# A two-layer hybrid attention stack: log gates by tokens, another order of heads and of competing PE lines

## Chip, cores, metric

One core of a Trainium2 chip. The metric is the device time of one execution in microseconds (us), median of the runs taken; the kernel before was run three times.

## The reference

Two layers over 1040 tokens (16 meta tokens and 1024 of `x`, width 1024, fp32). Each layer normalises the residual stream, projects it to 3588 columns and mixes three branches:

```python
log_f = log_sigmoid(fg + b_f[l])                    # forget gates, 4 heads
c = cumsum(log_f, axis=1)
a_out = forgetting_attention(fq, fk, fv, c) * silu(fz)      # scores + c[q] - c[k], causal
b_out = rmsnorm(differential_attention(dq, dk, dv, lam), subln_g[l]) * (1 - lambda_init) * silu(dz)
c_out = pooling_mixer(pu, w_pool[l], pool_scale[l]) * silu(pz)   # means of 2, 4, 8, 16 tokens
h = h + concat(a_out, b_out, c_out) @ w_out[l]
```

There are four forget heads of 64 columns and four difference heads (two score maps each, softmaxes subtracted with a factor `lam`). The output is `rmsnorm(h[16:], final_g)`.

## The kernel before

Every product is made of fp32r halves (a rounded part and the rest) in two or three matmuls, so PE does three passes for a projection. A layer runs as a stream of projections (`projections`, `proj_chunk`, three column chunks of about 346 tokens) in which the attention of six **units** is woven: two forget pairs (units 0 and 1, two heads each) and four difference heads (2 to 5). `UNITS` (L38) gives their order. While the attention of one unit runs, the V, Q and K projections of the next unit and the gate Z of this one are computed; in the last unit's time the two pooling items (`pool_item`, `pooling`) and their gates stand in the list `more` (L1525 to L1535).

The normalised tokens are transposed by PE (`to_hnT`, L584) into the tile `HT`. At the start `load_x` loads the token tiles (`x`), `load_g` the norm's factors (`g`), `rms` multiplies by both, and `forget_gates` (L722) computes the gates of layer 0 from `HT` with the split weights `wg`. For layer 1 the gates are made token by token in `next_gates` (L743): DVE multiplies each normalised row with the four gate columns `gw`, the sums land in `gt` (128 tokens x 9 x 4), nine PE transposes bring them into the row tile `gx` (4 partitions x 1040), and `gate_sums` (L773) takes the logarithm of the sigmoid and the running sum on those 4 partitions: minimum, a combination, Exp, Ln, a subtraction, a memset, a scan. The sums go to DRAM (`c_d`), and each forget pair reads its two rows back, broadcast to 128 partitions (`cb`).

What sets the order of the work: all operations but the PE's lines are recorded by `Timed` (so nearly all rows of ACT, DVE, POOL and SP bear L151), and `Order` lists them again. PE has up to six lines (`stream`: projections, scores, sums, transposes of V, start), each in fixed order; `Order.simulate` picks at every step, for every engine, the instruction that can start first by a table of costs (`Order.cost`), with the longest remaining way as a tie-break, and `Order.tell` writes that order into the program. On each engine instructions then run strictly in that order, and SP's queue (the DMA issues) too. PSUM has two banks `psP` for projections, three `psS` for scores, two `psT` for transposes, one `psO`. The SBUF ring `row` has eight buffers for `cb`, `sz`, `rq`, long softmax rows `p` and others.

`pooling` (L1189) makes window sums on DVE (`wa`, `wb`, `hd`), `pool_mix` (L1215) multiplies with `wps` on PE and evicts with the scale `sc`, a small DMA of its own. `meta_t` (L1002) copies the meta part of a weight block into `ptm`: ACT, DVE, ACT.

## Time and profile before

| | us |
|---|---|
| median of 3 runs (1224.27 to 1226.64) | 1224.74 |
| the profiled execution | 1224.48 |
| its span | 1222.7 |
| PE busy | 1188.7 (97%) |
| DVE, ACT, POOL busy | 814.0, 658.3, 493.5 |

The span is what the profiler shows from the first to the last instruction; the profiled execution is 1.8 us longer. PE's busy time counts a matmul from its start to a modelled end, so short delays between matmuls don't show as idle time, and idle time of other engines costs nothing by itself. The granted clock of PE was 0.998 of full speed over the span.

### The profile page before, as it was taken

What the parts mean: (1) busy time and instruction counts of PE and PEld (TensorE: products, weight loads), DVE (VectorE), ACT (ScalarE), POOL (GpSimd) and SP (SyncE); (2) the same over time, 40 slices, a digit from 0 to 9 for tenths busy, and PEclk for the clock granted to TensorE, in tenths of its full rate; (3) what the DMA queues carried; (4) which work ended last, traced back from release to release, by engine and by line L of the source; (5) the groups of instructions that cost most, each with busy time, mean ns of one, the idle gap of its engine ahead of it and who ended that gap; (6) DMA issues with size and microseconds to landing.
All of it is one profiled execution on the core that took longest, in us unless ns stands there. A gap on an engine that the chain in (4) does not pass through costs nothing.

```text
span 1222.7 us, 21035 instructions
## 1 busy us (share of the span) xinstructions
PE 1188.7 (97%) x7605; PEld 1120.7 (92%) x7605; DVE 814.0 (67%) x2137; ACT 658.3 (54%) x1536; POOL 493.5 (40%) x572
## 2 busy tenths in 40 slices
PE   5999999999999999899999999999999999999997
PEld 4999999999999999878889899999999999998886
DVE  6557567675766767667886675676768585777422
ACT  6556556565555654552235565665655555556322
POOL 4331623336162542465425234252443526235532
PEclk9999999999999999999999999999999999999999
DMA  7120211121222263472110212111223223325431
GB/s 244 27 71 18 59 47 27 45 44 32 53 40 61 35 126 78 136 237 80 67 53 18 71 36 69 27 27 53 30 42 61 40 50 65 78 50 158 140 108 52
DMA packets 101273, 84.21 MB, mean 69 GB/s; under 512 B 18296, under 2 KB 90232, under 8 KB 101168
## 3 DMA queue, kind: packets, MB, share of 16 engines
q1 hardware_dynamic: 101024, 82.60, 26.5%
q8 instruction: 60, 0.98, 0.3%
q14 instruction: 45, 0.37, 0.1%
q10 hardware_dynamic: 144, 0.26, 0.1%
HBM read 69.00 MB, written 13.80 MB: 68 GB/s over the span
## 4 chain that ended last, share of the span: by engine, by line
PE 86%; DVE 5%; ACT 3%; DMA 2%; issue 2%; SPq 1%; POOL 1%; POOLq 0%; ACTq 0%; DVEq 0%
PE psP L517 55%; PE psS L517 15%; PE psO L517 8%; PE psT L523 7%; DVE p L151 1%; SPq L151 1%; DMA r_d<-rs 1%; PE psS L523 1%; PE psT L517 1%; ACT K L151 1%; DVE K L151 1%; DMA sc<-in_pool_scale_dram 1%; ACT ptm L151 0%; DMA x<-in_x_dram 0%; DVE ptm L151 0%
## 5 line engine op out<-in xcount | busy, mean ns | idle before, releaser
L517 PE MATMUL psP<-HT,ws 128*128 128x346 f32 (+5 forms) x4032 | 730.3, 325 | 3.9 <-DVE K L151 2.0
L517 PEld LDWEIGHTS psP<-HT,ws 128*128 128x128 f32 x4032 | 636.5, 188 | 6.5 <-issue 2.3
L151 POOL TENSOR_TENSOR ws<-wr,ws 128x512 fp32r<-128x512 f32 x112 | 150.0, 1342 | 263.3 <-ACT ws L151 203.0
L151 POOL TENSOR_TENSOR q<-rq,q 64x256 fp32r<-64x256 f32 (+1 forms) x192 | 147.9, 770 | 124.7 <-DVE q L151 104.2
L151 ACT ACTIVATE p<-p,mx 128x144 f32<-128x144 f32 (+3 forms) x192 | 150.5, 784 | 49.3 <-DVE mx L151 48.3
L517 PE MATMUL psS<-K,q 128*128 128x392 f32 (+9 forms) x696 | 146.7, 324 | 1.0 <-DVE mx L151 0.8
L151 DVE TENSOR_TENSOR pp<-psT,pp 128x512 fp32r<-128x512 f32 (+1 forms) x160 | 99.2, 634 | 46.7 <-ACT pp L151 45.0
L517 PE MATMUL psO<-pp,VV 128*128 128x256 f32 (+1 forms) x800 | 129.2, 283 | 0.2
L523 PE MATMUL psT<-identf,p 128*128 128x128 f32 (+1 forms) x704 | 114.5, 273 | 3.3 <-DVE p L151 3.0
L151 ACT ACTIVATE pp<-psT 128x512 fp32r<-128x512 f32 (+1 forms) x160 | 85.4, 551 | 60.0 <-PE psT L523 55.9
L517 PE MATMUL psP<-HT,ms 128*128 128x512 f32 (+1 forms) x504 | 115.0, 385 | 0.5 <-POOL ms L151 0.3
L517 PEld LDWEIGHTS psO<-pp,VV 128*128 128x128 f32 x800 | 113.1, 189 | 2.0 <-DVE pp L151 0.9
L517 PEld LDWEIGHTS psS<-K,q 128*128 128x128 f32 (+1 forms) x696 | 108.4, 186 | 4.7 <-DVE mx L151 2.7
L517 PEld LDWEIGHTS psP<-HT,ms 128*128 128x128 f32 x504 | 90.7, 188 | 20.7 <-POOL ms L151 0.8
L523 PEld LDWEIGHTS psT<-identf,p 128*128 128x128 f32 (+1 forms) x704 | 81.3, 132 | 10.8 <-DVE p L151 4.7
L151 ACT ACTIVATE ws<-wr 128x512 fp32r<-128x512 f32 x112 | 70.0, 628 | 33.4 <-PE psP L517 18.4
L151 ACT ACTIVATE ptm<-psT 32x256 fp32r<-32x256 f32 (+1 forms) x128 | 47.5, 371 | 63.1 <-DVE ptm L151 45.0
L517 PE MATMUL psS<-HT,ms 128*128 128x512 f32 (+2 forms) x320 | 75.4, 394 | 0.0
L151 DVE TENSOR_SCALAR p<-p,rd 128x144 f32<-128x144 f32 (+7 forms) x128 | 72.3, 568 | 1.7
L517 PEld LDWEIGHTS psS<-HT,ms 128*128 128x128 f32 (+2 forms) x320 | 57.5, 180 | 16.7
L151 DVE TENSOR_TENSOR K<-psP,K 64x346 fp32r<-64x346 f32 (+1 forms) x72 | 37.2, 517 | 47.4 <-ACT K L151 46.8
L151 POOL TENSOR_TENSOR ms<-mr,ms 128x128 fp32r<-128x128 f32 (+2 forms) x39 | 39.1, 1010 | 68.7 <-ACT ms L151 68.6
(138 smaller groups left out, 1423.0 us busy)
## 6 DMA issues: line engine op xcount, KB each, us to landing
wr<-in_w_in_dram SPq DMA_DIRECT2D x112, 256.0 KB, 2.8
wo<-in_w_out_dram SPq DMA_DIRECT2D x14, 512.0 KB, 5.3
mr<-mix_d SPq DMA_DIRECT2D x14, 320.0 KB, 4.5
cb<-c_d SPq DMA_DIRECT2D x8, 520.0 KB
x<-in_x_dram SPq DMA_DIRECT2D x8, 512.0 KB, 6.5
res<-in_x_dram SPq DMA_DIRECT2D x8, 512.0 KB
h_d<-res SPq DMA_DIRECT2D x8, 512.0 KB, 2.6
res<-h_d SPq DMA_DIRECT2D x8, 512.0 KB, 4.6
```

Of the source, the lines that this page charges most:

```text
L151: r = f(*args, **kw)
L517: r = nc.tensor.matmul(o, w, m, start=start, stop=stop)
L523: r = nc.tensor.transpose(o, src, ident)
```

## The change

- In `next_gates` (layer 1) the logarithm is taken on the token-major tile `gt` (128 x 36) ahead of the transposes: bias, minimum, combination, Exp, Ln, subtraction. Only the scan stays on 4 x 1040, its ones are a constant, and the bias `bf` is loaded broadcast to 128 partitions. `gate_sums` still serves layer 0.
- The first `x` tile is asked for ahead of `g` (`load_x(2)` ahead of `load_g`).
- `UNITS` becomes (0, 2, 1, 3, 4, 5): a difference head between the two forget pairs, in both layers.
- In the last unit's list the first pooling item stands ahead of the unit's gate, the second behind it.
- `Order`: where PE's lines compete, the head that would be ready 400 ns (`SPARE`) later is compared, not the earliest; the scan's cost is 2.1 ns an element; writes to `ptm` count as writes to the whole tile, and in `meta_t` both ACT copies now stand ahead of the DVE subtraction; the list is made six times with new remaining ways, and the one that ends first by the table is kept (`choose`).

```diff
--- before.py
+++ after.py
@@ -35,7 +35,7 @@
 SLOPES = (2.0 ** -2, 2.0 ** -4, 2.0 ** -6, 2.0 ** -8)
 CHUNKS = ((0, 348), (348, 346), (694, 346))
 OWN_CHUNKS = (CHUNKS, ((META, 348 - META), *CHUNKS[1:]))
-UNITS = (0, 1, 2, 3, 4, 5)
+UNITS = (0, 2, 1, 3, 4, 5)
 V_CHUNKS = ((0, 400), (400, 384), (784, 256))
 FQ, FK, FV, FZ, FG = 0, 256, 512, 768, 1024
 DQ, DK, DV, DZ = 1028, 1540, 2052, 2564
@@ -166,6 +166,8 @@
 
     HOP = {"pe": 200, "act": 38, "dve": 38, "pool": 38, "dma": 0}
 
+    SPARE = 400
+
     def __init__(self):
         self.ops, self.writes, self.reads, self.rings, self.place = [], {}, {}, {}, {}
         self.stream = 0
@@ -208,7 +210,7 @@
                 name = ap.tensor.name
                 names.add(name)
                 p0, p1, at = self.parts(ap)
-                if self.place.get(name, ("",))[0] == "VM":
+                if self.place.get(name, ("",))[0] in ("VM", "ptm"):
                     p0, p1, at = 0, 128, [(0, 1 << 20)]
                 for lo, hi in at:
                     for other in others:
@@ -250,7 +252,9 @@
             return 158 + 1.05 * n + 63 * pointers, False
         if op == "reciprocal":
             return 157, False
-        if not sbuf or op == "tensor_tensor_scan":
+        if op == "tensor_tensor_scan":
+            return 150 + 2.1 * n, True
+        if not sbuf:
             return 150 + 1.05 * n, False
         if op == "tensor_copy" or op == "tensor_scalar":
             if len(ins[0].ap) > len(out.ap) or any(d[0] == 0 for d in ins[0].ap):
@@ -274,25 +278,36 @@
         for o in ops:
             for b in o["before"]:
                 ops[b]["after"].append(o["k"])
-
-        last = None
-        for o in reversed(ops):
-            way = max((ops[a]["way"] for a in o["after"]), default=0.0)
-            for n in o["tiles"]:
-                tag, i = self.place[n]
-                bufs, names = self.rings[tag]
-                if i + bufs < len(names) and self.first[names[i + bufs]] > o["k"]:
-                    way = max(way, ops[self.first[names[i + bufs]]]["way"])
-            way += o["end"]
+        self.start, self.heir = None, {}
+        for bufs, names in self.rings.values():
+            self.heir.update(zip(names, names[bufs:]))
+
+    def weigh(self):
+
+        ops, last = self.ops, None
+        for o in reversed(ops if self.start is None else sorted(ops, key=lambda o: (self.start[o["k"]], o["k"]))):
+            after = o["after"] + [self.first[self.heir[n]] for n in o["tiles"] if n in self.heir]
+            way = max((ops[a].get("way", 0.0) for a in after), default=0.0) + o["end"]
             if o["eng"] == "pe":
                 if last is not None:
                     way = max(way, last + o["dur"])
                 last = way
             o["way"] = way
 
+    def choose(self, rounds):
+
+        self.prepare()
+        best = None
+        for _ in range(rounds):
+            self.weigh()
+            end = self.simulate()
+            if best is None or end < best[0]:
+                best = end, self.start, self.done, self.taken, self.order
+            self.heir = {old: n for n, old in self.taken.items() if old}
+        _, self.start, self.done, self.taken, self.order = best
+
     def simulate(self):
         ops = self.ops
-        self.prepare()
         left = [len(o["before"]) for o in ops]
         ready = [0.0] * len(ops)
         start, done = [None] * len(ops), [None] * len(ops)
@@ -347,11 +362,13 @@
                         if not line or left[line[-1]] or (s := slots(line[-1])) is None:
                             continue
                         t = max(free["pe"], ready[line[-1]] + 20, s + 20)
-                        d = (t, 0.0, line[-1], t, e)
+                        sure = max(free["pe"], ready[line[-1]] + self.SPARE, s + self.SPARE)
+                        d = (sure, 0.0, line[-1], t, e)
                         if c is None or d < c:
                             c = d
                     if c is None:
                         continue
+                    c = (c[3], *c[1:])
                 else:
                     c = None
                     for k in waiting[e]:
@@ -742,14 +759,14 @@
 
     def next_gates(l):
 
-        bf = small.tile([4, 1], F32, tag="bf", name=nm("bf"), bufs=2)
-        sync.dma_start(bf, b_f[l].rearrange("(f o) -> f o", o=1))
-        gx = row("gx")[:4]
+        bf = small.tile([128, 4], F32, tag="bfr", name=nm("bf"), bufs=1)
+        sync.dma_start(bf, b_f[l].partition_broadcast(128))
         gw = [sb.tile([128, D], F32, tag="q", name=nm("gw"), bufs=4) for _ in range(4)]
         for f in range(4):
             sync.dma_start(gw[f], c_wg[l, f].partition_broadcast(128))
 
         gt = small.tile([128, 9, 4], F32, tag="gt", name=nm("gt"), bufs=1)
+        dve.memset(gt, 0.0)
         done = []
 
         def rows(hn, np_, col):
@@ -761,12 +778,24 @@
             done.append((g, np_, col))
 
         def end():
+            gx = row("gx")[:4]
+            flat = gt.rearrange("p n f -> p (n f)")
+            mn = sm("mn", 36)
+            dve.tensor_tensor(out=gt, in0=gt, in1=bf.unsqueeze(1).to_broadcast([128, 9, 4]), op=ALU.add)
+            dve.tensor_scalar(out=mn, in0=flat, scalar1=0.0, scalar2=None, op0=ALU.min)
+            dve.scalar_tensor_tensor(out=flat, in0=mn, scalar=2.0, in1=flat, op0=ALU.mult, op1=ALU.subtract)
+            act.activation(flat, flat, AF.Exp)
+            act.activation(flat, flat, AF.Ln, bias=1.0)
+            dve.tensor_tensor(out=flat, in0=flat, in1=mn, op=ALU.subtract)
             with ordr.line(4):
                 for g, np_, col in done:
                     pt = psT()[:4, :np_]
                     transpose(pt, g, identf[:np_, :np_])
-                    act.activation(gx[:, col : col + np_], pt, AF.Identity, bias=bf)
-            gate_sums(l, gx)
+                    act.activation(gx[:, col : col + np_], pt, AF.Copy)
+            mn = row("mn")[:4]
+            dve.tensor_tensor_scan(
+                out=mn, data0=one[:4].to_broadcast([4, T]), data1=gx, initial=0.0, op0=ALU.mult, op1=ALU.add)
+            sync.dma_start(c_d[l], mn)
 
         return rows, end
 
@@ -1007,8 +1036,8 @@
                 transpose(pt[:, b + 128 * i : b + 128 * i + 128], P[2 * jp + i][:, 0:32], identf)
             ptm = keep["m"] = small.tile([96, 272], F32R, tag="ptm", name=nm("ptm"), bufs=2)[:, :nq]
             act.activation(ptm[0:32], pt, AF.Copy)
+            act.activation(ptm[64:96], pt, AF.Copy)
             dve.tensor_tensor(out=ptm[32:64], in0=pt, in1=f32(ptm[0:32]), op=ALU.subtract)
-            act.activation(ptm[64:96], pt, AF.Copy)
 
         def out_tile():
             if "O" not in keep:
@@ -1464,6 +1493,7 @@
         act.dma_start(out[0, t0 : t0 + 128, 512:], res[:, 512:])
 
     HT = big.tile([128, 2, 8, T], F32R, name="HT")
+    load_x(2)
     g = load_g(norm_g[0])
     load_x(5)
     hns = []
@@ -1530,7 +1560,7 @@
                 more += nxt
             else:
                 Y = []
-                more += [pool_item(l, t, Y) for t in (1, 0)] + [pool_gate(l, t, Y) for t in (1, 0)]
+                more = [pool_item(l, 1, Y), *more, pool_item(l, 0, Y)] + [pool_gate(l, t, Y) for t in (1, 0)]
                 raw = []
                 more[-1] = (*more[-1][:4], lambda: (w_out_loads(l, raw, 4), raw.append(first_mix(l))))
             unit_steps(cur, end, len(more) * tile_ns + (LAG if u == 5 else 0))
@@ -1546,7 +1576,7 @@
         plan.run(op, 14 * 3 * 216)
         for _ in op:
             pass
-    ordr.simulate()
+    ordr.choose(6)
     ordr.tell(tc)
 
 _INS = ("x", "meta_tokens", "norm_g", "w_in", "b_f", "lam_q1", "lam_k1", "lam_q2", "lam_k2",
```

What this does to the order, at three places.

**The start, PE** (matmuls of the gate chunk of layer 0 write psP_296; `identf,x_104` and `identf,x_157` are transposes of the fourth and fifth token tile; `psP_330` is the first V chunk). Before:

```order
L523 MATMUL psS_282<-identf,x_104 128x128 x4
L523 MATMUL psS_289<-identf,x_104 128x128 x4
L523 MATMUL psS_316<-identf,x_157 128x128 x2
L517 MATMUL psP_296<-HT,wg_138 36x348 x16
L523 MATMUL psS_316<-identf,x_157 128x128 x2
L523 MATMUL psS_323<-identf,x_157 128x128 x4
```

Now:

```order
L540 MATMUL psS_282<-identf,x_104 128x128 x4
L540 MATMUL psS_289<-identf,x_104 128x128 x4
L534 MATMUL psP_296<-HT,wg_138 36x348 x16
L534 MATMUL psP_330<-HT,ws_149 128x400 x12
L534 MATMUL psP_330<-HT,ws_154 128x400
L540 MATMUL psS_316<-identf,x_157 128x128 x4
L540 MATMUL psS_323<-identf,x_157 128x128 x4
```

The gate chunk no longer stands behind two transposes of the fifth tile. On **DVE** at the same place, before:

```order
L151 TENSOR_TENSOR HT<-psS_275,HT 128x4x128
L151 CAST wg_138<-wrg_139 128x8x4
L151 SCALAR_TENSOR_TENSOR x_157<-x_157,rs_177,g_96 128x1024
L151 TENSOR_TENSOR wg_138<-wrg_139,wg_138 128x8x4
L151 TENSOR_TENSOR HT<-psS_282,HT 128x4x128
L151 TENSOR_TENSOR HT<-psS_289,HT 128x4x128
```

Now:

```order
L151 SCALAR_TENSOR_TENSOR x_104<-x_104,rs_166,g_98 128x1024
L151 CAST wg_138<-wrg_139 128x8x4
L151 TENSOR_TENSOR wg_138<-wrg_139,wg_138 128x8x4
L151 TENSOR_TENSOR HT<-psS_282,HT 128x4x128
L151 TENSOR_TENSOR HT<-psS_289,HT 128x4x128
L151 SCALAR_TENSOR_TENSOR x_157<-x_157,rs_177,g_98 128x1024
```

The split of `wg` moved ahead of the normalisation of the fifth tile `x_157`; that of the fourth, `x_104`, moved behind two more subtractions for `HT`.

**Layer 1's gates, DVE** (mn, na, gx: the row tiles of `gate_sums`; K0, K1: eviction of a K chunk from psP). Before:

```order
L151 TENSOR_SCALAR mn_7967<-gx_6828 4x1040
L151 SCALAR_TENSOR_TENSOR na_7969<-mn_7967,gx_6828 4x1040
L151 TENSOR_TENSOR K_1666_8034<-psP_8082,K_1666_8034 64x346
L151 MEMSET gx_6828 4x1040
L151 TENSOR_TENSOR K_1667_8035<-psP_8082,K_1667_8035 64x346
L151 TENSOR_TENSOR na_7969<-na_7969,mn_7967 4x1040
L151 TENSOR_TENSOR K_1666_8034<-psP_8111,K_1666_8034 64x346
L151 SCALAR_TENSOR_TENSOR mn_7967<-gx_6828,na_7969 4x1040
L151 TENSOR_TENSOR K_1667_8035<-psP_8111,K_1667_8035 64x346
```

Now (gt: the token-major tile; the row with `one` is the scan):

```order
L151 SCALAR_TENSOR_TENSOR gt_6836<-mn_7941,gt_6836 128x36
L151 TENSOR_TENSOR gt_6836<-gt_6836,mn_7941 128x36
L151 CAST q_7987<-rq_7685 64x256 x2
L151 CAST q_7996<-rq_7685 64x256 x2
L151 TENSOR_TENSOR K_1666_8035<-psP_8047,K_1666_8035 64x348
L151 TENSOR_TENSOR K_1667_8036<-psP_8047,K_1667_8036 64x348
L151 TENSOR_TENSOR VV_7683<-psT_8054,VV_7683 128x2x64 x2
L151 SCALAR_TENSOR_TENSOR mn_7975<-one,gx_7940 4x1040
L151 TENSOR_TENSOR K_1666_8035<-psP_8083,K_1666_8035 64x346
L151 TENSOR_TENSOR K_1667_8036<-psP_8083,K_1667_8036 64x346
L151 CAST q_8005<-rq_7685 64x256 x2
```

Of the 4 x 1040 operations the scan alone is left, and it stands ahead of the second K chunk instead of inside the third.

**The pooling of layer 0, SP** (sc: the scale of a pooling item; r_d and vr: a trip of norm factors through DRAM; wo: output weights). Before:

```order
L151 DMA wp_6486<-in_w_pool_dram 64x64 x2
L151 DMA r_d<-rs_1367_6270 128x2
L151 DMA wo_6767<-in_w_out_dram 128x512
L151 DMA vr_6346<-r_d 128x256
L151 DMA sc_6343<-in_pool_scale_dram 128x1
L151 DMA sc_6493<-in_pool_scale_dram 128x1
L151 DMA wo_6768<-in_w_out_dram 128x512
```

Now, the first scale:

```order
L151 DMA wr_6084<-in_w_in_dram 128x4x128
L151 DMA wr_6089<-in_w_in_dram 128x4x128
L151 DMA sc_6063<-in_pool_scale_dram 128x1
L151 DMA wr_6414<-in_w_in_dram 128x4x128
L151 DMA wr_6419<-in_w_in_dram 128x4x128
```

and the second:

```order
L151 DMA vr_6322<-r_d 128x272
L151 DMA r_d<-rs_1367_6268 128x2
L151 DMA wo_6767<-in_w_out_dram 128x512
L151 DMA vr_6356<-r_d 128x256
L151 DMA sc_6493<-in_pool_scale_dram 128x1
L151 DMA wo_6768<-in_w_out_dram 128x512
```

The first scale stands ahead of the weights of the pooling gates, far ahead of the trips through r_d; the second still stands behind one.

## Rows read from the trace of the kernel before

**Rows 1.** Page, first part: busy time of each engine, share of the span, instructions.

```profile
PE 1188.7 (97%) x7605; PEld 1120.7 (92%) x7605; DVE 814.0 (67%) x2137; ACT 658.3 (54%) x1536; POOL 493.5 (40%) x572
```

**Rows 2.** Busy time by stretch: length, busy PE, PEld, DVE, ACT, POOL (instructions), granted clock, DMA.

```profile
19.00:22.40 3.40, 0.57 (x5) 0.36 (x4) 3.40 (x4) 2.52 (x5) 3.24 (x4) 1.00 0.58 167
...
22.40:26.60 4.20, 4.20 (x18) 2.76 (x18) 1.03 (x2) 0.63 (x1) 2.60 (x3) 0.59 0.72 198
...
40.00:490.00 450.00, 447.69 (x3043) 435.66 (x3042) 308.28 (x940) 262.32 (x622) 176.22 (x186) 1.00 0.23 52
...
490.00:550.00 60.00, 56.44 (x329) 48.13 (x327) 36.98 (x73) 34.04 (x83) 33.52 (x40) 1.00 0.61 186
...
672.00:690.00 18.00, 15.72 (x105) 15.04 (x103) 8.83 (x23) 9.53 (x21) 5.60 (x4) 1.00 0.34 105
...
690.00:1085.00 395.00, 392.97 (x2682) 383.45 (x2681) 280.30 (x814) 233.18 (x544) 149.88 (x166) 1.00 0.22 47
...
1085.00:1120.00 35.00, 32.71 (x219) 31.82 (x218) 25.96 (x58) 20.34 (x41) 16.29 (x15) 1.00 0.38 106
...
1120.00:1222.70 102.70, 96.03 (x456) 79.27 (x454) 36.42 (x49) 31.06 (x82) 38.21 (x65) 0.99 0.35 109
```

**Rows 3.** Timeline of the first 40 us: start, length, engine, operation, count, idle before.

```profile
5.76 1.27 DVE L151 SCALAR_TENSOR_TENSOR x<-x,rs,g 16x1024 f32<-16x1024 f32 x1 [3.72 <-DMA g<-in_norm_g_dram]
...
7.09 1.06 ACT L151 ACTIVATE junk<-x 128x1024 bf16<-128x1024 f32 x1 [3.15 <-DMA x<-in_x_dram]
...
10.10 4.69 PE L523 MATMUL psS<-identf,x 16*128 16x16 f32 x24 [10.10 <-DMA identf<-in_ident_dram]
...
18.80 1.07 DVE L151 CAST wg<-wrg 128x32 fp32r<-128x32 f32 x1
...
19.78 2.35 DVE L151 SCALAR_TENSOR_TENSOR x<-x,rs,g 128x1024 f32<-128x1024 f32 x1
...
22.27 0.51 PE L523 MATMUL psS<-identf,x 128*128 128x128 f32 x2 [2.83 <-DVE wg L151]
...
22.44 4.33 PE L517 MATMUL psP<-HT,wg 128*36 128x348 f32 x16
...
37.13 2.74 PE L517 MATMUL psP<-HT,wg 128*36 128x346 f32 x16
```

**Rows 4.** Timeline around layer 1's gates: DVE, then PE.

```profile
673.84 1.23 DVE L151 TENSOR_TENSOR na<-na,mn 4x1040 f32<-4x1040 f32 x1 [2.78 <-ACT na L151]
...
675.64 2.31 DVE L151 TENSOR_TENSOR_SCAN mn<-gx,na 4x1040 f32<-4x1040 f32 x1
...
678.65 7.53 PE L517 MATMUL psP<-HT,ws 128*128 128x346 f32 x46 [2.03 <-DVE K L151]
```

**Rows 5.** Chain that ended last, 660 to 700 us: start, length, piece.

```profile
679.47 2.42 DMA c_d<-mn
...
681.91 4.02 DMA cb<-c_d
```

**Rows 6.** Chain that ended last, 490 to 530 us.

```profile
488.31 5.26 DMA r_d<-rs
...
494.00 2.91 DMA sc<-in_pool_scale_dram
```

**Rows 7.** Timeline at the two pooling stages: PE, then DVE and PE.

```profile
497.73 0.75 PE L517 MATMUL psP<-pu,wps 128*128 128x346 f32 x3 [1.21 <-ACT Y L151]
...
511.18 1.86 PE L517 MATMUL psP<-HT,ws 128*128 128x348 f32 x10 [1.53 <-DVE th L151]
...
1104.35 4.14 DVE L151 SCALAR_TENSOR_TENSOR p<-p,n,p 128x912 f32<-128x912 f32 x2
...
1108.55 0.55 PE L523 MATMUL psT<-identf,p 128*128 128x128 f32 x3 [1.83 <-DVE p L151]
```

**Rows 8.** Waits of the whole span: who for whom, us in total, times, longest.

```profile
ACT ptm L151 <- DVE ptm L151: 45.0, 63, 1.8
...
PEld psO L517 <- ACT ptm L151: 4.2, 13, 0.5
```

## The prediction

> **What bounds the kernel now.** I read the page's first part first: PE is busy for 1188.7 of 1222.7 us, the next engine (DVE) for 814.0 [rows 1]. Before and after the change PE has the same products and transposes to do, so the only time to be had is PE's idle time, 1222.7 − 1188.7 = 34.0 us, and what PE does at the lower clock. The second view is busy time by stretch, to see where those 34.0 us lie [rows 2]. 10.1 us come before the first transpose [rows 3]; the stretch 19.0 to 22.4 lacks 2.83; the two attention stretches 40 to 490 and 690 to 1085 lack only 2.31 and 2.03 in 845 us together; the end of layer 0 (490 to 550) lacks 3.56, layer 1's gates (672 to 690) 2.28, the end of layer 1 (1085 to 1120) 2.29, and the tail from 1120 lacks 6.67. The change touches the tail in nothing. So what it can reach is 2.83 + 3.56 + 2.28 + 2.29 = 10.96 us at the four seams, some 4.3 inside the attention, and the clock in the head. Third I read the timeline at the four seams [rows 3, 4, 7], for what each wait waits for; fourth the chain of waits, for the DMAs behind them [rows 5, 6]; last the waits of the whole span, for the work on `ptm` [rows 8].
>
> The sum is made against the profiled execution, 1224.48 us, 1.8 above its span and 0.3 below the median of the runs. A measurement of this kernel can tell about 0.2% (2.4 us) from no change.
>
> **Part by part.**
>
> *x ahead of g: 0.* The first rows are multiplied at 5.76, when `g` lands; the first full tile of `x` lands only for 7.09. Now the two change places, so `g` should come some 7.09 − 5.76 = 1.3 later and `x` earlier by as much. But PE's first transposes start at 10.10 because of `identf` [rows 3], which stands behind the same transfers in either order. The multiplication of 16 rows takes 1.27; begun at 7.1 it ends at 8.4, still 1.7 ahead of `identf`, which is the cover. If that were gone, it would cost the 1.3 at most.
>
> *The gate chunk of layer 0 comes earlier: −2.0 (bounds −2.8 and −0.7).* PE waits 2.83 us up to 22.27, by the profile for `wg` (the split by DVE); then it does two transposes of the fifth tile and the 16 gate matmuls [rows 3]. The cast of `wg` ends at 18.80 + 1.07 = 19.87, and only behind it stands the multiplication of `x_157`, 2.35 long, 19.78 to 22.13: the second half of `wg`, and `x_157` itself, wait for that. In the new order both operations on `wg` stand ahead of `x_157`, and PE's gate chunk ahead of its transposes. The second half of the split is 128 x 32; the nearest price is the cast of the same tile, 1.07; anything from near 0 to that. So the gate chunk could start between 19.9 and 21.0 in place of 22.44. The multiplication of the fourth tile, `x_104`, now stands closer ahead of the split (nearest row: 1.27), so it could be put off by 1.27 more. Lower bound 22.44 − 20.94 − 0.8 = 0.7, upper 2.8 (the whole wait); I take 2.0, nearest to a short second half. What is gained stays gained: from 22.4 to 26.6 PE is busy without a gap (4.20 of 4.20).
>
> *Layer 1's gates: −2.2 (bounds −2.5 and −1.0).* On DVE the 4 x 1040 subtraction (1.23, which first idled 2.78 for ACT's Ln) and the scan (2.31) stand among the evictions of K; PE waits 2.03 at 678.65 for the last of them [rows 4]. Now combination, Exp, Ln and subtraction are 36 wide, and the memset is gone; the scan is left, one chunk earlier and without a wait for ACT in front of it. New are a memset of `gt`, an addition with a stretched operand, and the bias loaded to 128 partitions, all well ahead and small: I set them at 0 under PE's products before 672 (PE is busy 15.72 of 18.0 there even with the wait). If that cover failed, six operations of 36 columns at under 1.23 each (the 1040-wide one) would be under 7.4, on engines with DVE 8.83 and ACT 9.53 busy of 18.0 [rows 2]. The 2.03 go, and up to 0.25 of the rest of the 2.28; the lower bound is a wait for the scan where it now stands: 2.31 less what the second K chunk covers.
>
> *Forget sums earlier: 0 for the first pair.* The sums' way through DRAM is 2.42 + 4.02 = 6.4 long and lies on the chain [rows 5]; with the narrow logarithm it starts earlier. That takes it off the chain and frees nothing more than the 2.03 above.
>
> *The pooling items: layer 0 −2.0 (bounds −3.6 and 0), layer 1 −1.3 (bounds −2.3 and 0).* The chain at layer 0's end runs through a trip of `rs` to DRAM, 5.26, and behind it in SP's queue the load of `sc`, 2.91 [rows 6]; ACT's eviction with `sc` holds a bank psP, and PE waits 1.21 for it at 497.73 and 1.53 for `th` (DVE) at 511.18 [rows 7]. In the new order the first `sc` is asked for far ahead of any trip, the second still behind one. So of the two items that compete with the last difference head one is out of the way: I take the 1.21 and half of the 1.53. In layer 1 two long softmax rows `p` of 4.14 together stand back to back on DVE, and PE's transposes wait 1.83 for them [rows 7]; with one item's window sums done earlier, DVE and POOL have less at that place: I take 1.3 of 2.29. The lower bound of both is 0: the first item now takes its DVE time inside the head, where PE lacks little, and could leave as much there.
>
> *`ptm`: −1.0 (bounds −4.2 and 0).* ACT waits 45.0 us in 63 waits for DVE's subtraction on `ptm`; PE's weight loads wait for the second copy 4.2 in all, 13 times, 0.5 at most [rows 8]. With both copies ahead of the subtraction ACT's wait goes; of the 4.2 much lies beside a running matmul (PEld overlaps PE). DVE reads `ptm[0:32]` after both copies rather than one, which is later by one ACT copy.
>
> *Units, `SPARE`, `choose`: +0.5 (bounds −2 and +2).* No operation is added. What a different order could win inside the two attention stretches is 2.31 + 2.03 [rows 2]. The same rows bound a loss loosely: 4.34 idle in 845 us says that the waits there are already covered, and a new order has as good a chance to uncover some. I take +0.5.
>
> Sum: −2.0 − 2.2 − 2.0 − 1.3 − 1.0 + 0.5 = −8.0; 1224.48 − 8.0 = **1216.5**.
>
> **A rule beside the rows: the clock in the head.** From 19.0 to 22.4 PE is busy 0.57 of 3.40 us, and from 22.4 to 26.6 the granted clock is 0.59: most of the gate chunk runs at 1.2 GHz, its 16 matmuls taking 4.33 where the next such chunk takes 2.74 at 37.13 [rows 2, 3]. My sum keeps that.
>
> The Trainium skill ("TensorE: Matmul & The Clock Gate", Part 1: The HAM clock gate) says that the half rate is the default and that the engine's activity releases it, an idle engine falling back. Here the trace agrees as far as it goes: a pause, then 0.59. By that rule a shorter pause could leave the clock at 2.4 GHz; that is rival (a).
>
> **The rivals.**
>
> (a) *The clock holds.* PE's pause shrinks from 2.83 to about 0.8, so the gate chunk runs as at 37.13: another 4.33 − 2.74 = 1.6 us, 1214.9. For it: after the pause the clock was low, and later, without pauses, 1.00. Against it: PE's start at 10.10 with narrow transposes is itself light work, and the pause is not gone.
>
> (b) *Only head and gates hold*, and the pooling waits move into the head that the item now shares: −2.0 − 2.2 = −4.2, 1220.3. For it: both stretches of pooling have several releasers (ACT, DVE) [rows 7], not one.
>
> (c) *The waits only change places.* In each seam the wait removed uncovers the next on the same engines (the scan before the K chunk, `x_157`'s transposes behind the gate chunk): about 1224, no change.
>
> (d) *Slower: the second pair's `cb` comes late.* Unit 1 now starts after a difference head, and its two `cb` loads move back in SP's queue by some sixteen places, behind weights and a trip through `r_d`; they take two of the eight `row` buffers at a time when the head's long rows want them. If SP reaches them later than 4.02 us (one landing) ahead of the pair's first scores, PE waits at each layer as at layer 1's start: about 2.3 idle and the 4.02 of a landing, 6.3; two layers 12.6. From 1216.5 that is 1229.1. It decides at those 4.02 us; the rest of the queue is light (DMA share 0.23 in 40 to 490 [rows 2]), which speaks against it.
>
> **How the numbers follow.** Forecast 0.45, (a) 0.17, (b) 0.14, (c) 0.14, (d) 0.10. Faster (below 1222.0) are the forecast, (a) and nearly all of (b): 0.74. The same is (c) with the upper edge of (b): 0.16. Slower is (d): 0.10. The range: downwards (a) with the seams' full idle time, 1214.9 − 1.6 − 1.0 − 0.8 (the rest of layer 0's 3.56, of layer 1's 2.29, of the head) = 1211.5, say 1211.0; upwards (b) and most of (c), 1224.0. Outside lie (d) and the edge of (c).
>
> **What would show it.** Head: the gate chunk of layer 0 starts near 20.4, not 22.44, and has 4.33 (clock low) or 2.74 (clock held). Gates: no wait of about 2 us for DVE's `K` around 676, and `cb` of layer 1 landing some us earlier against the first scores. Pooling: `sc` out of the chain that ended last, idle PE in the last 60 us of layer 0 below 2. `ptm`: ACT's 45.0 us of waits gone, PEld's 4.2 smaller. Wrong I would be if PE's idle time inside the attention stretches rose above some 7 us, or if `cb` of unit 1 appears as a releaser of PE.

## The result

| | before | after |
|---|---|---|
| median us (4 runs each) | 1225.24 | 1208.85 |
| ratio, 95% interval | | 0.9865 [0.9847, 0.9882] |
| span of the profiled execution | 1222.7 | 1206.8 |
| PE busy; idle | 1188.7; 34.0 | 1178.5; 28.3 |
| PEld busy; idle | 1120.7; 102.0 | 1120.1; 86.7 |

(Idle is the span less the busy time.) The change saves 16.4 us, twice the 8.0 forecast and outside the range of 1211 to 1224. The first part of the page of the changed kernel, which answers to [rows 1]:

```profile
PE 1178.5 (98%) x7605; PEld 1120.1 (93%) x7605; DVE 805.6 (67%) x2138; ACT 658.7 (55%) x1536; POOL 491.3 (41%) x572
```

The span shrank by 15.9. PE's idle time gave 5.7 of that; **10.2 came out of PE's busy time**, with the same 7605 matmuls. The weight loads' idle time fell by 15.3: that row saw nearly all of it.

Where it came from, by places that both kernels pass. Timeline of PE of the kernel before, the first output products of layer 0, the first transposes of layer 1's gates, the first output products of layer 1:

```profile
528.49 0.92 PE L517 MATMUL psP<-HT,ms 128*128 128x512 f32 x3
...
658.97 0.37 PE L523 MATMUL psT<-identf,gt 128*4 128x128 f32 x2
...
1125.82 0.92 PE L517 MATMUL psP<-HT,ms 128*128 128x512 f32 x3
```

The same in the changed kernel:

```profile
521.96 1.73 PE L534 MATMUL psP<-HT,ms 128*128 128x512 f32 x6 [0.20 <-ACT ms L151]
...
651.12 0.37 PE L540 MATMUL psT<-identf,gt 128*4 128x128 f32 x2
...
1109.57 0.86 PE L534 MATMUL psP<-HT,ms 128*128 128x512 f32 x3
```

With the second gate chunk (37.13 in [rows 3], 35.94 below) and the spans:

| stretch | forecast | measured |
|---|---|---|
| head, to the second gate chunk | -2.0 | -1.2 |
| layer 0, attention and pooling | -2.25 | -5.3 |
| to the first gate transposes of layer 1 | 0 | -1.3 |
| layer 1, gates, attention, pooling | -3.75 | -8.4 |
| the rest | 0 | +0.3 |

(The forecast's 1.0 for `ptm` and 0.5 for the order are halved between the layers.) Busy time by stretch in the changed kernel; columns as in [rows 2], the bounds moved by what had been gained:

```profile
19.00:22.40 3.40, 2.92 (x13) 2.48 (x14) 1.62 (x5) 2.66 (x5) 3.15 (x5) 0.50 0.54 172
22.40:26.60 4.20, 4.20 (x21) 3.24 (x20) 2.29 (x4) 1.80 (x4) 3.14 (x3) 0.76 0.73 199
40.00:484.00 444.00, 440.65 (x3013) 431.39 (x3013) 305.50 (x927) 262.50 (x620) 174.63 (x187) 1.00 0.22 51
484.00:544.00 60.00, 59.80 (x353) 52.24 (x352) 41.07 (x85) 34.60 (x83) 30.49 (x39) 1.00 0.67 195
664.00:682.00 18.00, 18.00 (x125) 17.92 (x124) 8.90 (x31) 10.73 (x26) 8.25 (x9) 1.00 0.34 110
682.00:1069.00 387.00, 382.93 (x2641) 377.35 (x2641) 273.17 (x797) 230.24 (x534) 151.70 (x167) 1.00 0.22 47
1069.00:1104.00 35.00, 35.00 (x238) 34.75 (x237) 27.92 (x64) 20.85 (x43) 13.12 (x13) 1.00 0.38 109
1104.00:1206.80 102.80, 96.13 (x458) 79.63 (x456) 34.55 (x48) 31.57 (x82) 36.77 (x65) 0.99 0.33 109
```

PE's idle time at the end of layer 0 fell from 3.56 to 0.20, at the gates from 2.28 to 0, at the end of layer 1 from 2.29 to 0: the three seams were emptied, 7.9 in all. Inside the two attention stretches it rose, 2.31 to 3.35 and 2.03 to 4.07, and yet these stretches became shorter. (The windows do not hold the same work, 3043 matmuls and 3013 in the first, but each matmul's share fell too: 147.9 to 147.4 ns, and 147.3 to 146.5 in layer 1.) Both parts of that contradiction matter below.

**Delays that the busy row hides.** Timeline of the kernel before, PE and then PEld:

```profile
150.06 0.37 PE L517 MATMUL psP<-HT,ws 128*128 128x346 f32 x1
150.53 0.38 PE L517 MATMUL psO<-ptm,VM 96*128 96x256 f32 x1
...
150.52 0.19 PEld L517 LDWEIGHTS psO<-ptm,VM 96*128 96x128 f32 x1 [0.34 <-ACT ptm L151]
```

The weights wait 0.34 us for ACT. The matmul starts 0.47 behind the one before it, three times the usual 0.16; but that one is shown for 0.37, so PE's row has 0.10 idle: 0.21 of the 0.31 lost are hidden. I took the starts of all matmuls from the traces, and from each distance the median for its number of columns and target bank in the kernel before. What is left over, added up by size:

| | 0.1 to 0.5 us | over 0.5 us |
|---|---|---|
| before | 19.1 | 15.9 |
| after | 9.6 | 11.4 |

Of 15.8 us between first and last matmul, 9.5 come from delays of 0.1 to 0.5 us, 4.5 from longer ones, and 1.7 from distances nearer to the median. Most of the short ones are hidden, not all: PE's row shows 4.2 us of them as idle time before, and 1.5 after. Matmuls at the lower clock fall into the same class, since they start 0.29 us apart where others of their size start 0.16 apart; in these two kernels that is 1.6 and 1.7 us, all in the gate chunk of the head, and so not what changed. A second profile of the changed kernel (`after2` below) has 9.5 us of short delays again, but 14.6 of longer ones: only the first class is repeatable to better than 3 us.

By place: the two attention stretches lost 7.3 us of short delays and took on 5.1 of longer ones; the three seams (in the kernel before 490 to 550, 659 to 690 and 1085 to 1120) lost 2.2 of short ones and all 7.8 of longer ones. With the distances nearer to the median, some 10 us of the 15.8 were won at the seams and some 3 in the attention.

The Trainium skill ("Perfetto Trace Analysis", Identifying the Most-Contended Engine) says that a matmul's busy share is a poor measure since matmuls are pipelined, and that the weight loads' busy share should be read instead. This trace agrees: PE busy fell by 10.2 with the same work, PEld busy by 0.6.

**The chain after.** Neither `sc` nor `cb` is on the changed kernel's chain at the places of [rows 5, 6]. The waits of the whole span, most of those of PE, then PEld and DVE:

```profile
PE psT L540 <- DVE p L151: 3.6, 2, 2.0
PE psS L534 <- DVE mx L151: 2.8, 3, 1.3
PE psS L540 <- DVE wg L151: 2.8, 1, 2.8
PE psS L540 <- DVE x L151: 0.9, 1, 0.9
PE psO L534 <- DVE ptm L151: 0.8, 2, 0.5
...
PEld psO L534 <- DVE ptm L151: 1.4, 2, 0.8
...
DVE sz L151 <- DMA vr<-r_d: 21.5, 13, 4.6
```

ACT's 45.0 us of waits for `ptm` [rows 8] are gone, and PEld's 4.2 are 1.4, now for DVE's subtraction. What has grown is the last row: DVE stood 6.9 us for `vr` in the kernel before, and stands 21.5 now.

### The profile page after: what moved, and what is told of

It reads as the page before. It is cut to its first block, busy times and chain, and to the rows that moved or that the text cites. A ratio compares the mean times of both kernels' runs of the same rounds, so it can differ in the third digit from the quotient of the medians.

```text
span 1206.8 us, 21081 instructions
## 1 busy us (share of the span) xinstructions
PE 1178.5 (98%) x7605; PEld 1120.1 (93%) x7605; DVE 805.6 (67%) x2138; ACT 658.7 (55%) x1536; POOL 491.3 (41%) x572
## 4 chain that ended last, share of the span: by engine, by line
PE 92%; DVE 2%; DMA 2%; ACT 1%; SPq 1%; issue 1%; POOL 0%; POOLq 0%; DVEq 0%; ACTq 0%
PE psP L534 60%; PE psS L534 15%; PE psO L534 8%; PE psT L540 7%; DMA vr<-r_d 1%; PE psS L540 1%; SPq L151 1%; DVE p L151 1%; PE psT L534 1%; DMA x<-in_x_dram 0%; DMA wp<-in_w_pool_dram 0%; DVE K L151 0%; ACT p L151 0%; DMA r_d<-rs 0%; ACT K L151 0%
## 5 line engine op out<-in xcount | busy, mean ns | idle before, releaser
L534 PE MATMUL psS<-K,q 128*128 128x328 f32 (+9 forms) x696 | 149.1, 324 | 2.8 <-DVE mx L151 2.8
L534 PEld LDWEIGHTS psP<-HT,ms 128*128 128x128 f32 x504 | 90.4, 188 | 20.6 <-issue 0.6
L151 DVE TENSOR_SCALAR p<-p,rd 128x784 f32<-128x784 f32 (+7 forms) x128 | 69.6, 545 | 1.4
L151 DVE CUSTOM_DVE_ANT_0 p<-psS,dist 128x272 f32<-128x272 f32 (+7 forms) x128 | 61.1, 490 | 10.3 <-PE psS L534 5.5
L151 ACT ACTIVATE ms<-mr 128x128 fp32r<-128x128 f32 (+2 forms) x40 | 16.3, 415 | 87.5 <-PE psS L534 34.1
```

The costliest lines, as they stand in the source:

```text
L151: r = f(*args, **kw)
L534: r = nc.tensor.matmul(o, w, m, start=start, stop=stop)
```

## The experiments

All ratios are to the kernel before on the same chip, with 95% intervals; the control `after2`, the changed kernel again, gives 0.9867, and chips differ by 0.2 to 0.3% in the times themselves. The table is for looking up. Delays as above, matmuls at the lower clock among the short ones; "vr" is DVE's wait for that DMA. Profiles are compared with that of the control.

| kernel | ratio | span | PE idle | PEld idle | 0.1 to 0.5 | over 0.5 | vr |
|---|---|---|---|---|---|---|---|
| before | 1 | 1222.7 | 34.0 | 102.0 | 19.1 | 15.9 | 6.9 |
| after2 | 0.9867 | 1210.4 | 31.3 | 90.3 | 9.5 | 14.6 | 28.5 |
| a_ptm | 0.9921 | 1215.2 | 32.1 | 94.7 | 14.2 | 14.0 | 27.0 |
| a_spare | 0.9976 | 1222.7 | 36.0 | 100.3 | 16.5 | 19.1 | 19.9 |
| a_spare250 | 0.9908 | 1214.0 | 33.2 | 94.3 | 11.6 | 16.3 | 20.7 |
| a_spare450 | 0.9913 | 1217.4 | 31.8 | 91.0 | 15.8 | 15.1 | 14.2 |
| a_units | 0.9865 | 1209.0 | 28.8 | 88.6 | 10.8 | 12.1 | 23.9 |
| a_gates | 0.9911 | 1214.6 | 32.9 | 92.9 | 11.3 | 16.8 | 26.6 |
| a_pool | 0.9928 | 1217.1 | 33.3 | 93.8 | 13.7 | 17.3 | 26.5 |
| a_head | 0.9896 | 1212.5 | 30.6 | 90.4 | 11.9 | 14.1 | 22.4 |
| a_choose2 | 0.9936 | 1220.0 | 35.8 | 95.6 | 13.9 | 19.3 | 17.4 |
| b_rules | 0.9955 | 1220.8 | 34.8 | 96.1 | 14.5 | 20.0 | 23.0 |
| b_parts | 1.0024 | 1230.3 | 37.0 | 106.6 | 22.1 | 19.1 | 12.2 |
| b_ptm | 1.0109 | 1241.7 | 48.1 | 115.7 | 19.7 | 33.7 | 15.1 |
| b_sp350 | 1.0000 | 1224.9 | 36.1 | 100.6 | 16.8 | 20.1 | 15.5 |
| v_dma | 0.9873 | 1208.2 | 28.3 | 86.3 | 9.5 | 12.6 | 2.4 |
| v_dma6 | 0.9860 | 1207.5 | 27.8 | 85.6 | 9.9 | 12.0 | 4.0 |
| v_trip | 0.9860 | 1205.4 | 27.4 | 85.5 | 8.8 | 10.5 | 3.1 |
| v_trip_p | 0.9841 | 1204.8 | 25.3 | 83.6 | 11.3 | 8.1 | 3.2 |

**One part undone at a time.** The control:

> The changed kernel again, as the control on the same chip as the next three: 0.9865 of the kernel before, PE busy near 1178.5, PEld idle near 86.7.

It gave 0.9867 [0.9852, 0.9882], PE busy 1179.1. The order on `ptm`:

```diff
-    if self.place.get(name, ("",))[0] in ("VM", "ptm"):
+    if self.place.get(name, ("",))[0] in ("VM",):
...
-            act.activation(ptm[64:96], pt, AF.Copy)
             dve.tensor_tensor(out=ptm[32:64], in0=pt, in1=f32(ptm[0:32]), op=ALU.subtract)
+            act.activation(ptm[64:96], pt, AF.Copy)
```

> The changed kernel with the work on ptm as before (copy, subtraction, copy; the parts of the tile tracked apart). Theory I (only PE time that the profile shows as idle can be won, as the forecast had it): PE busy stays at 1178.5 and the time rises by the forecast's 1.0, to about 1209.8. Theory H (delays of 0.1 to 0.5 us between matmuls are counted as busy, since a matmul is shown for some 0.3 us and the next one starts some 0.16 later): PE busy rises by 2 to 4 and PE idle by under 1, PEld idle rises by 3 to 5, time 1212 to 1214, and ACT's 45 us of waits for DVE's ptm are back.

0.9921 [0.9897, 0.9946], 6.6 us more than the control. PE busy rises by 4.0, PE idle by 0.8 and PEld idle by 4.4, all three as theory H had it; ACT waits 44.4 again. The time rises by more than H's 3 to 5. In the profiles the whole loss lies in layer 1: from the gate transposes to the output products it takes 464.8 us against the control's 459.9, while layer 0 takes 487.6 against 487.7, though ACT waits 22 us in either layer. So ACT's wait by itself does not make the loss; that this list lets it reach PE in layer 1 is likely, not shown.

The margin, `SPARE = 20`:

> The changed kernel with SPARE at 20 ns instead of 400, which compares the heads of PE's lines by their earliest start, as before. Theory I: no effect beyond 1 us, 1208 to 1210. Theory H: the short delays come back, PE busy up by 4 to 6 with PE idle up by under 2, PEld idle up by 5 to 7, time 1214 to 1216.

0.9976 [0.9962, 0.9990], 13 us more than the control: five sixths of the whole gain go with this one number. PE busy rises by 7.6, PE idle by 4.7, and the two classes of delay by 7.0 and 4.5 (1.6 of the 7.0 are matmuls at the lower clock, behind a wait at 356 us). Theory I falls; H has the direction, but not the size, and not the long waits.

The units, `UNITS = (0, 1, 2, 3, 4, 5)`:

> The changed kernel with the units in the order 0, 1, 2, 3, 4, 5 again. Theory I (the units' order only moves waits): 1208 to 1210. Rival U (the difference head between the two forget pairs spreads DVE's and ACT's work, and is worth a good part of what the forecast missed): 1212 to 1216, with more waits for p, mx and s in 40 to 200 us and in 690 to 850.

0.9865 [0.9841, 0.9889]: no difference, to within 3 us. Rival U falls.

The gates, the old `next_gates`:

> The changed kernel with the gates of layer 1 made as before (logarithm on 4 x 1040 behind the transposes). The forecast's term: +2.2, 1211.0, with a wait for DVE's K of about 2 us at layer 1's first chunks. Rival: the new order hides most of the long operations without the narrow ones, +0.5 or less, 1209.

0.9911 [0.9889, 0.9933], 5.4 us more; PE's list is the changed kernel's in all of layer 0, so the loss belongs to layer 1. Timeline of PE in that kernel:

```profile
671.32 9.86 PE L534 MATMUL psP<-HT,ws 128*128 128x346 f32 x59 [1.19 <-DVE K L151]
...
682.53 0.52 PE L534 MATMUL psS<-K,q 128*128 128x272 f32 x2 [1.35 <-DVE mx L151]
```

The first wait is the one forecast, only shorter. The second was not: DVE stood 1.94 for `cb` just ahead of it. So the late running sums do cost PE time, 2.5 in the two together; the rest of the 5.4 lies in later waits of layer 1.

The pooling items, in their old order:

```diff
-  more = [pool_item(l, 1, Y), *more, pool_item(l, 0, Y)] + [pool_gate(l, t, Y) for t in (1, 0)]
+  more += [pool_item(l, t, Y) for t in (1, 0)] + [pool_gate(l, t, Y) for t in (1, 0)]
```

> The changed kernel with both pooling items behind the last head's projections and the gate, as before. The forecast's terms: +2.0 in layer 0 and +1.3 in layer 1, 1212.2, with waits for Y or th near 490 to 520 and for p near 1090. Rival: below 1 us, because ptm and the margin have freed ACT and PE there.

0.9928 [0.9911, 0.9946], 7.5 us more, and all of it in layer 1 (in layer 0 the 60 us from 490 lack 0.26). Timeline of PE, then busy time by stretch:

```profile
1087.48 0.36 PE L534 MATMUL psT<-s,onesr 128*128 128x256 f32 x1 [1.26 <-DVE s L151]
1089.16 0.58 PE L534 MATMUL psT<-s,onesr 128*128 128x256 f32 x1 [1.33 <-POOL s L151]
...
1092.37 2.10 PE L534 MATMUL psP<-HT,ws 128*128 128x346 f32 x6 [2.63 <-ACT Y L151]
```

```profile
1075.00:1110.00 35.00, 29.12 (x175) 28.09 (x174) 19.82 (x43) 18.28 (x41) 17.43 (x20) 0.85 0.41 109
```

A chain of waits over DVE, POOL and ACT leaves PE idle for 5.9 of 35 us, and the granted clock is 0.85 over the stretch: 0.50 from 1090 to 1095 us and 0.68 in the next 5, which PE works through without a gap. The pause is paid a second time.

The loads, without `load_x(2)`:

> The changed kernel with g loaded ahead of the first x tile again. Forecast: 0, and the gain of the head (1.0 measured up to the second gate chunk) stays. Rival: the order of the loads is what brings the head's gain: +1 to +3, in the first 40 us.

0.9896 [0.9881, 0.9911], 3.6 us more. Its matmuls stand in another order than the changed kernel's at 30 of 7605 places, all among the first 99, so this is the load order and what the list makes of it. Timeline of PE:

```profile
24.80 4.20 PE L534 MATMUL psP<-HT,wg 128*36 128x348 f32 x16 [1.82 <-DVE wg L151]
```

The gate chunk starts at 24.80, later than in the kernel before (22.44). The forecast's 0 was wrong.

**More lists, other margins.** `choose(2)` in place of 6, and two margins:

> The changed kernel with two lists tried instead of six (the list with the remaining ways weighed again once is taken). The table puts little between the second and the sixth: within 2 us of the control at 0.9867, 1209 to 1212. Rival C: the chip tells lists apart that the table does not, 3 us or more away on either side.

> The changed kernel with SPARE 250 instead of 400 (20 gave 0.9976 of the kernel before against 0.9865). Theory H (the margin keeps PE from waits of some tenths of a microsecond that the list does not foresee): most of the gain is there at 250, within 4 us of the control, 1209 to 1213 on a chip like the first. Rival C (another margin only draws another list, and what a list is worth is chance): anywhere between the control and a_spare, 1209 to 1223, with the gain lost in a few long waits at other places.

> The changed kernel with a margin of 450 ns in place of 400, a number with no reason behind it. Theory H alone: as the control, within 2 us (0.985 to 0.989). Rival C (which list comes out is worth several microseconds by chance): 3 us or more from the control, with new long waits at places where the control has none.

0.9936 [0.9921, 0.9951], 0.9908 [0.9894, 0.9923], 0.9913 [0.9896, 0.9929]: 8.5, 5.0 and 5.6 us worse than the control. Rival C is right about the size: 450 for 400 has no reason behind it and costs about as much as `ptm`, the gates or the pooling order. One place where it costs, in the timeline of a_spare450, DVE, then PE:

```profile
444.27 0.23 DVE L151 CAST wps<-wp 128x128 fp32r<-128x128 f32 x1 [4.39 <-DMA wp<-in_w_pool_dram]
...
446.66 1.25 PE L534 MATMUL psS<-K,q 128*128 128x144 f32 x4 [2.60 <-DVE mx L151]
```

DVE, which runs strictly in order, stands 4.39 us at a small copy whose DMA has not landed; the eviction of `K` and a maximum behind it wait, and so does PE. The wait is not the whole price: the granted clock is 0.60 from 445 to 450 us and 0.72 from 450 to 455, with matmuls 0.29 us apart in place of 0.16; and it is 0.83 from 350 to 360 and 0.66 from 540 to 545. The control has 1.00 in all four. That is why this kernel has hardly more long delays than the control (15.1 and 14.6) but 15.8 us of short ones against 9.5: rival C's new long waits came only in part, and the clock behind waits is the other part. In a_choose2 too the clock is 0.91 from 340 to 360 and 0.83 from 500 to 520, both behind waits. How much of each loss is the clock's was not separated.

**Parts on the kernel before.** The rules alone (order, costs, margin, lists, `ptm`), the program's parts alone, `ptm` alone, the margin alone:

> The rules of the list and the order on ptm alone (margin 400, ptm as one tile with both copies first, the scan's cost, six lists), on the program of before: the head, layer 1's gates, the units' order and the pooling items as in the kernel before. Forecast: -1.0 + 0.5 = -0.5 against the kernel before, 1224. Theory H: -5 to -9 (0.993 to 0.996 of before), with PE busy down by 4 to 7 and PEld idle down by 6 to 9. If every part's loss just adds up (ptm 6.8 and margin 13.5 from the runs without them) it would be -20, 1204.

> The program's parts alone (first x tile ahead of g, narrow gates of layer 1, the units' order, the first pooling item ahead of the gate) under the rules of the list as they were (margin 20 ns, ptm in parts with its old order, the scan's old cost, one list). Forecast, by its terms: -2.0 - 2.2 - 2.0 - 1.3 = -7.5, 0.994 of before. The rules alone gave 0.9955, so if rules and parts only add up this run gives 0.991, -11. If each needs the other, it stays between 0.994 and 1.000, with long waits left where the list does not foresee them.

> The kernel before with the order on ptm alone (one tile, both ACT copies ahead of DVE's subtraction). Forecast: -1.0 (bounds 0 and -4.2). Theory H: -3 to -5, with PE busy down by 2 to 4, PE idle by under 1.5, the PEld wait of 4.2 for ptm down to under 1.5, and ACT's 45 us of waits for ptm gone. Rival C: another list, anywhere from -3 to +3, whatever becomes of the waits for ptm.

> The kernel before with the margin alone, at 350 ns. Forecast: between -2 and +2. Theory H: -4 to -8, the delays of 0.1 to 0.5 us fewer, PE busy down by 3 to 6. Rival: the margin is worth little without the other parts, since the long waits (gates, pooling) stay: -2 to 0.

0.9955 [0.9940, 0.9970], 1.0024 [1.0009, 1.0039], 1.0109 [1.0094, 1.0124], 1.0000 [0.9989, 1.0011]. None gives what its undoing costs, two are slower, and rules and parts add to -0.2%, not to -1.3%. The margin alone does take 2.3 us out of the delays of 0.1 to 0.5 us, and 4.2 of longer ones appear. `ptm` alone is worst; timeline, ACT's second copy, DVE's subtraction, PE:

```profile
1108.24 0.37 ACT L151 ACTIVATE ptm<-psT 32x256 fp32r<-32x256 f32 x1
...
1112.42 0.41 DVE L151 TENSOR_TENSOR ptm<-psT,ptm 32x256 fp32r<-32x256 f32 x1
...
1112.98 0.55 PE L517 MATMUL psO<-ptm,VM 96*128 96x256 f32 x1 [5.45 <-ACT p L151]
```

ACT is freed of its wait, but DVE's subtraction is now the last of the three. Here it stands 4 us behind pooling work and long combinations in DVE's queue, and PE behind it. (The view puts PE's wait down to ACT's `p`, which ended within 0.1 us of the subtraction; the matmul reads `ptm`.) In the changed kernel, where the first pooling item comes earlier, PE loses nothing in these last 35 us: a place where one part needs another.

**Telling the list the truth.** The long waits left in the changed kernel have one pattern. Timeline of the control, DVE, then PE:

```profile
452.97 0.49 DVE L151 SCALAR_TENSOR_TENSOR sz<-sz,gs,vr 128x256 f32<-128x256 f32 x1 [2.08 <-DMA vr<-r_d]
453.49 0.43 DVE L151 TENSOR_TENSOR ptm<-psT,ptm 32x272 fp32r<-32x272 f32 x1
...
453.98 0.40 PE L534 MATMUL psO<-ptm,VM 96*128 96x272 f32 x1 [1.49 <-DVE ptm L151]
```

`vr` comes 2 us later than the table counts on. Four kernels change the table's costs of DMAs (in `note`); v_dma:

```diff
-  more = 1600 if inps[0].ap[0][0] == 0 else 1100 if out.ap[-1][1] < 8 else 0
+  more = 2300 if inps[0].ap[0][0] == 0 else 1900 if out.ap[-1][1] < 8 else 0
```

and v_dma6 with 2000 in both places:

> The changed kernel with one number of the list's table set nearer to what the traces show: 0.7 us more for a DMA that is read broadcast (vr), 0.8 more for a narrow one (rs, r_d). Theory V (the long waits left in the changed kernel, at about 352, 382, 453 and 1035 us, come from DVE standing at sz for vr, which lands some 2 us later than the list counts on, with mx, ptm and K queued behind): DVE's wait for vr falls from 21 to 28 us to under 12, three of these waits go, 4 to 6 us are won against the control, 0.982 to 0.984 of before. Rival C (another number only draws another list): no better than the control, 0.985 to 0.995.

> The same with 0.4 us more for the broadcast DMA and 0.9 more for the narrow one: another list with nearly the same knowledge. Theory V: within 2 us of v_dma. Rival C: 4 us or more apart from it.

0.9873 [0.9858, 0.9888] and 0.9860 [0.9845, 0.9875]; DVE's wait for `vr` falls to 2.4 and 4.0, PE's waits for `ptm` are gone, and those for `mx` fall from 3.5 to 1.2 us. But the time did not follow: 0.7 us worse and 0.9 better than the control, where theory V had 4 to 6 won. The broadcast and narrow loads of the start got the new costs too, and its list changed: up to the second gate chunk the two are 2.2 and 3.3 us behind the changed kernel. So the other two keep the old costs there:

```diff
+  if "r_d" in inps[0].tensor.name:
+      more = 2300
+  elif "r_d" in out.tensor.name:
+      more = 2400
```

> The changed kernel with the list's costs raised for the trip through r_d alone (1.3 us more for rs to r_d, 0.7 more for vr), so that the list of the start stays as in the changed kernel. Theory V: the head's loss of v_dma and v_dma6 (2.2 to 3.4 us against the changed kernel up to the second gate chunk) is gone, DVE's wait for vr stays under 6 us, and the time is 2 to 4 us below theirs: 0.983 to 0.985 of before. Rival C: 0.986 or more, with long waits at new places.

> The same, and the longest combination of a difference head (p, 128 x 1040) costs 2.2 us in the table instead of 1.3, since two of the eight took 2.3 beside POOL's work and PE waited 2.0 and 1.7 us behind them. Theory V: these two waits (about 352 and 800 us) shrink below 1 us each, another 2 to 3 us: 0.981 to 0.983. Rival C: not better than v_trip by more than 1 us, or worse.

v_trip: 0.9860 [0.9845, 0.9875]; v_trip_p, which also gives the longest `p` 2.2 us: **0.9841 [0.9825, 0.9858]**, the best of all. PE's two waits for `p` are 1.2 and 0.6, against 2.0 and 1.6 in the changed kernel. The gains against the control are 0.9 and 3.2 us. v_trip's is smaller than expected, within the noise, and its time is one that rival C allowed. v_trip_p is 2.3 us below v_trip, as theory V had it, and PE's waits for `p` are 1.8 us in all against v_trip's 3.8, one of them still over the 1 us that was expected. Still each is another list, its interval just touches the control's, and lists have differed by 5 us without a reason: that the truer costs make the 3.2 us is likely, not shown.

## Why the prediction was wrong

The direction was right; the size failed at two steps, the short delays left out and the seams priced too low, and the parts' prices at more.

- **"The only time to be had is PE's idle time, 1222.7 − 1188.7 = 34.0 us"** is the step that failed. There were 19.1 us in delays of 0.1 to 0.5 us, of which PE's row shows only 4.2 as idle, and 9.5 of the 19.1 went; 10.2 of the 15.9 us came out of busy time. The text ahead of the prediction even said that short delays don't show as idle time; the sum was made as if they did not exist. The attention stretches could therefore shrink while their idle time grew. That growth, from 4.3 to 7.4, is past the "some 7 us" that the prediction named as a sign of being wrong: the new order did uncover longer waits there, 5.1 us of them, and the 7.3 of short delays that went outweighed them.
- **"Units, `SPARE`, `choose`: +0.5 (bounds -2 and +2)."** The bound came from the same idle time. Undone in the changed kernel, the margin costs 13 us and the lists 8.5; the units cost nothing that the runs can tell. On the kernel before, the margin gave nothing. They have no price of their own.
- **The head, -2.0**: -1.2 at the second gate chunk; the first starts at 21.07, not near 20.4. The split of `wg` ended at 19.64, near the forecast, its second half 0.19 long. But the eight transposes of the fourth tile, ahead of the chunk, came only then, 1.94 long. Timeline, DVE, then PE, of the changed kernel (with [rows 3]):

```profile
7.24 2.47 DVE L151 SCALAR_TENSOR_TENSOR x<-x,rs,g 16x1024 f32<-16x1024 f32 x2 [5.23 <-DMA g<-in_norm_g_dram]
...
19.25 0.17 DVE L151 CAST wg<-wrg 128x32 fp32r<-128x32 f32 x1
19.45 0.19 DVE L151 TENSOR_TENSOR wg<-wrg,wg 128x32 fp32r<-128x32 f32 x1
...
19.48 1.94 PE L540 MATMUL psS<-identf,x 128*128 128x128 f32 x8 [2.76 <-DVE wg L151]
21.07 4.31 PE L534 MATMUL psP<-HT,wg 128*36 128x348 f32 x16
...
35.94 2.74 PE L534 MATMUL psP<-HT,wg 128*36 128x346 f32 x16
```

  PE's pause is 2.76, not 0.8; it only ended earlier. Rival (a), the held clock, did not come: the granted clock was 0.50 and 0.76 in the stretches above, and the chunk took 4.31.
- **x ahead of g, 0**: wrong. `g` came 1.5 later, near the forecast's 1.3, two multiplications followed it at once and ended at 9.71, and `identf` (9.96) still covered them, by 0.25 and not 1.7. But without the swap the gate chunk falls back to 24.80.
- **The gates, -2.2**: the mechanism was right. Timeline, DVE, then PE (with [rows 4]):

```profile
648.65 0.20 DVE L151 TENSOR_TENSOR gt<-gt,mn 128x36 f32<-128x36 f32 x1 [1.84 <-ACT gt L151]
...
659.12 2.30 DVE L151 TENSOR_TENSOR_SCAN mn<-one,gx 4x1040 f32<-4x1040 f32 x1
...
656.89 9.04 PE L534 MATMUL psP<-HT,ws 128*128 128x346 f32 x56
```

  The subtraction went from 1.23 to 0.20, the scan kept 2.30, and PE's K chunks run through without a wait. What was missed is `cb`: "frees nothing more than the 2.03" holds no longer once a_gates shows 1.35 behind it.
- **Pooling, -2.0 and -1.3**: mis-sized. The seams gave 3.4 and 2.3 of idle time, at the upper bounds. With the gates the forecast took 5.5 us at the three seams; they gave 7.9 of idle time and 2.2 of short delays. `sc` left the chain as forecast.
- **`ptm`, -1.0**: ACT's waits went as forecast; the price was not the change's own. Alone it costs 13 us, in part for a reason named in that step (DVE reads after both copies, "later by one ACT copy") and priced at nothing: the cost is not the copy but the work that may stand ahead of a later place in DVE's queue. In b_ptm four matmuls on `ptm` start 1.0 to 5.6 us late, 9.8 in all; in the kernel before none is over 0.5. The rest of the 13 is another list and the lower clock behind its waits (0.85 from 1110 to 1145).
- **Rival (d)** did not come: in the changed kernel DVE waits once for `cb`, 1.7, at layer 1's first pair, and PE not at all. Rivals (b) and (c), at 1220.3 and 1224, are excluded by the time.

Shown is where the 16.4 us lie; not settled is how they divide among the parts. Undoing them one by one costs 13 + 8.5 + 7.5 + 6.6 + 5.4 + 3.6 + 0, some 45 us in all, and another margin without a reason costs 5.6. A cost of that size shows a part's worth only where the trace has its wait at its own place (gates, pooling, head); for the margin and the number of lists it was only argued that they find a list in which few such places collide. That six lists and 400 ns gave a good one is in part luck: 450 ns, against which nothing spoke beforehand, gave one that is 5.6 us worse.

## What to carry to other kernels

Where matmuls are pipelined, judge headroom by the distances between starts or by the idle time of the weight loads; the busy row hides of each delay what a matmul is shown for beyond its usual distance. Look at the granted clock behind every long wait, too: the wait can be paid twice. Where a program's order is made by a table, one part's effect can't be read from one run: undo it, apply it alone, and change a number that should not matter, to learn how far lists differ. Then look for engines that stand at a late DMA with others queued behind, and give the table the measured trip.

## What was not expected

- Of the eight longest combinations of `p` (128 x 1040) in the changed kernel three take 2.3 to 2.4 us and one 1.9, the others 1.3. Timeline of POOL, DVE, PE around one:

```profile
348.76 2.62 POOL L151 TENSOR_TENSOR ws<-wr,ws 128x512 fp32r<-128x512 f32 x2 [1.42 <-issue]
...
350.10 2.37 DVE L151 SCALAR_TENSOR_TENSOR p<-p,n,p 128x1040 f32<-128x1040 f32 x1
...
352.53 0.98 PE L540 MATMUL psT<-identf,p 128*128 128x128 f32 x7 [1.97 <-DVE p L151]
```

  DVE's instruction ends 1.1 us behind the end of POOL's second one (351.38). A POOL instruction stands beside all eight. Beside the four long ones it started from 0.10 us ahead of DVE's to 0.04 behind; beside the four short ones 0.22 us or more behind, and there POOL's is the long one: `s<-sq,s` took 1.63 to 1.66 us beside three of them, and 0.74 beside the combination of 1.9. So whichever starts first goes through, and the other waits. The Trainium skill ("SBUF — State Buffer", Who interferes with whom) says that a DVE instruction with two SBUF inputs contends with a POOL instruction that reads SBUF, and that the pair of ports they share is an exclusive lock. This trace agrees, though no run took POOL's work away.
- In a_ptm PE paused for 2.70 us at the same place in the head as the changed kernel (2.76), and the row of the granted clock shows 1.00 before and after, where the changed kernel has 0.50. Yet the matmuls of its gate chunk start 0.29 us apart up to 24.1 us, as in the changed kernel at 0.50, and 0.16 apart from 24.5 on; the chunk took 3.73, not the 2.74 of [rows 3]. So in the head the lower level can be there while the row shows full speed, and the distances between starts are to be read with it. In a_pool and a_spare, with the same matmuls up to there, the chunk took 3.31 and 4.79: where in it the clock rises differs from one execution to the next.
